# One plain pair of column blocks less in each feed-forward, and two sums moved ahead, in a two-layer hybrid decoder trunk

## The chip, the core and the metric

The kernel runs on one core of a Trainium2 chip. Its time is the device time of one execution in microseconds (us); lower is better. The five engines of the core have a queue each and run it in order: TensorE (PE) multiplies, VectorE (DVE) does elementwise work, ScalarE (ACT) activations and copies, GpSimd (POOL) some DMAs and a few splits, SyncE (SP) issues most DMAs.

## What is computed

Two layers on 512 tokens of width 1024, float32. Each layer is a feed-forward, a mixer and a feed-forward, each between two RMS norms:

```python
def swiglu(x, w_gate, w_up, w_down):
    return (jax.nn.silu(x @ w_gate) * (x @ w_up)) @ w_down
...
for layer in range(DEPTH):
    f = swiglu(rmsnorm(h, nw[0]), ffn_w_gate[layer, 0], ffn_w_up[layer, 0], ffn_w_down[layer, 0])
    h = h + FFN_RES_SCALE * rmsnorm(f, nw[1])
    u = rmsnorm(h, nw[2])
    m = even_mixer(u, ...) if layer % 2 == 0 else odd_mixer(u, ...)
    h = h + rmsnorm(m, nw[3])
    f = swiglu(rmsnorm(h, nw[4]), ffn_w_gate[layer, 1], ffn_w_up[layer, 1], ffn_w_down[layer, 1])
    h = h + FFN_RES_SCALE * rmsnorm(f, nw[5])
```

The inner width of a feed-forward is 2816, 22 column blocks of 128. The even mixer is windowed attention beside a gated delta rule, the odd one a Mamba-2 scan; the change touches neither.

## The kernel before, in words

Products are made in three passes: every operand is split into a high part (hi, made by a cast on ACT) and the rest (lo, a subtraction on DVE), and hi·hi, hi·lo and lo·hi are summed. `split` (L76 to L81) does this: the cast and the subtraction both carry lines L80 and L81. The input of a feed-forward, the normed and transposed tokens, is `uT`, a pair of tiles uhi and ulo of 128 x 4 token tiles x 8 x 128, filled by `pre` token tile by token tile as the sub-layer before ends.

`ffn` makes gate and up in three kinds of work, one behind the other:

- **Early blocks**: the first two column blocks. Each has a gate and an up product; all four run first on tokens 0 to 255, then on tokens 256 to 511 (`product`, L167 to L169, 128x256), since the last token tiles come late. `finish` (L322, L323) applies Silu and multiplies, and its result is a half of an h tile.
- **Plain blocks**: the next two column blocks, four products on all 512 tokens, 96 matmuls of 512 columns (L167 to L169).
- **Strassen units**: the rest, two column blocks at a time (gate and up of two blocks, as a 2x2 block product by seven multiplications). `block_product` (L292 to L302, matmuls at L300) is one multiplication, 24 matmuls of 256 columns, so a unit has 168. Their left operands are A11, A12, A22 (quarters of uT) and S1 to S4, sums and differences of the quarters, each with its own hi and lo. S1 to S4 are made once for each feed-forward: four sums of hi and lo (`whole`, L352), a subtraction (L362), three combinations (L363, L366, L369), four splits (s1, s2, s3, and S4, which takes the place of a quarter of uT, so its lo is called ulo). r11, r12, r21 and r22 are h tiles that aren't used yet.

A unit's weights are five loads of 512 KB: b11, t1 and t3 into the pool wq (five buffers), b21 and b22 into wraw (three). t1 and t3 are differences that an accumulating DMA of POOL (L380) makes on top of a first load by SP (L378). The block products in order: b11 with A11; b21 with A12; b11' = t1 + b22 (the `add` at L388) with S2; t1 with S1; t3 with S3; b22 with S4; b21' = b11' + b21 with A22. Each operand goes through `forms`, which splits it into whi (ACT) and wlo (DVE), four buffers of each. The q tiles hold partial results.

The order on each engine isn't written by hand: a scheduler at build time places the instructions by the order of the code and by when their inputs would be ready. On the chip each queue then runs in that order. The even mixer gives every fifth weight split to POOL, by a running count of `weights` calls (L88 to L96).

Below, the four feed-forwards are numbered first to fourth in order of time.

Of the kernel before, what the change touches and what calls it, by code (L numbers as in the profile page):

```python
# [30 lines left out]
class Trunk:  # L31
# [272 lines left out]
    def ffn(self, w_gate, w_up, w_down, post_w, next_pre, raws={}):  # L304
# [3 lines left out]
        nf = w_gate.shape[1] // 128  # L308
        tt, stt = nc.vector.tensor_tensor, nc.vector.scalar_tensor_tensor
        with ExitStack() as ctx:  # L310
            hp = ctx.enter_context(self.tc.tile_pool(name="ffn_h", bufs=1, reuse_waits="tile"))

            place = lambda dt=F32: hp.tile([128, 2, T], dt, name="h", bufs=nf // 2)
            early, plain = 2, 2
            acc, wts, hT = {}, {}, []
            with ExitStack() as ctx2:
                pool = lambda name, **kw: ctx2.enter_context(self.tc.tile_pool(name=name, reuse_waits="tile", **kw))
# [2 lines left out]
                def finish(f):  # L320
                    s = self.scratch()
                    nc.scalar.activation(s, acc[f, 0], AF.Silu)  # L322
                    tt(hT[f // 2][:, f % 2, :], acc[f, 1], s, op=OP.mult)  # L323

                r11, r12, r21, r22 = (place().rearrange("p f (k c) -> p f k c", c=128) for _ in range(4))
                for f in range(early):
                    for g, w in ((0, w_gate), (1, w_up)):
                        wts[f, g] = self.w_cols(w, f * 128, raw=raws.get((f, g)))
                        acc[f, g] = self.ps("acc" if f else "mm")
                        self.product(acc[f, g][:, :256], wts[f, g], 0, 2)  # L330
                for f in range(early):
                    for g in range(2):
                        self.product(acc[f, g][:, 256:], wts[f, g], 2, 4)
                    if f == 0:
                        hT.append(place())
                    finish(f)

                for f in range(early, early + plain):
                    if f % 2 == 0:
                        hT.append(place())  # L340
                    for g, w in ((0, w_gate), (1, w_up)):
                        acc[f, g] = self.ps("mm")
                        self.product(acc[f, g], self.w_cols(w, f * 128))
                    finish(f)


                half = lambda i, j: [u[:, 2 * i:2 * i + 2, 4 * j:4 * j + 4, :] for u in self.uT]
                A11, A12, A21, A22 = (half(i, j) for i in range(2) for j in range(2))
                flat = lambda x: x.rearrange("p t k c -> p t (k c)")

                def whole(r, x):
                    tt(flat(r), flat(x[0]).bitcast(F32), flat(x[1]).bitcast(F32), op=OP.add)  # L352

                def parts(r, x):
                    self.split(flat(r), *(flat(y) for y in x))
                    return x

                new = lambda n: [sp.tile([128, 2, KD // 2, 128], F32R, name=n + x) for x in ("hi", "lo")]
                whole(r11, A11)
                whole(r21, A21)  # L360
                whole(r22, A22)
                tt(flat(r21), flat(r22), flat(r21), op=OP.subtract)  # L362
                stt(flat(r11), flat(r21), -1.0, flat(r11), op0=OP.mult, op1=OP.subtract)  # L363
                S2 = parts(r11, new("s2"))
                S1n = parts(r21, new("s1"))
                stt(flat(r22), flat(r11), -1.0, flat(r22), op0=OP.mult, op1=OP.subtract)  # L366
                S3 = parts(r22, new("s3"))
                whole(r12, A12)
                stt(flat(r12), flat(r11), -1.0, flat(r12), op0=OP.mult, op1=OP.subtract)  # L369
                S4 = parts(r12, A21)  # L370

                def unit(f, pool, name, *parts):

                    raw = pool.tile([128, KD // 2, 256], F32, name=name)
                    for i, (w, k) in enumerate(parts):
                        src = w[k * 128:(k + KD // 2) * 128, f * 128:(f + 2) * 128].rearrange("(k p) c -> p k c", p=128)
                        if i == 0:
                            nc.sync.dma_start(raw, src)  # L378
                        else:
                            nc.gpsimd.dma_start(raw, src, accum_op=OP.add)  # L380
                    return raw

                def forms(raw):
                    hi, lo = (self.wsplit.tile([128, KD // 2, 256], F32R, name=x) for x in ("whi", "wlo"))
                    self.split(raw, hi, lo)
                    return hi, lo
# [2 lines left out]
                q = lambda n: qp.tile([128, 512], F32, name=n)  # L389

                two = lambda x: x.rearrange("p (f t) -> p f t", f=2)
                for f in range(early + plain, nf, 2):
                    b11, b21 = unit(f, wq, "wq", (w_gate, 0)), unit(f, self.wraw, "wraw", (w_gate, 4))
                    t1 = unit(f, wq, "wq", (w_gate, 0), (w_up, 0))
                    b22 = unit(f, self.wraw, "wraw", (w_up, 4))
                    t3 = unit(f, wq, "wq", (w_up, 4), (w_up, 0))
                    a = self.ps("mm")
                    self.block_product(a, forms(b11), A11, True)
                    q1 = q("q1")
                    nc.scalar.copy(q1, a)  # L400
                    c = self.ps("acc")
                    self.block_product(c, forms(b21), A12, True)
                    add(q1, c, q1)
                    nc.scalar.activation(q1, q1, AF.Silu)
                    add(b11, t1, b22)
                    self.block_product(a, forms(b11), S2, False)
                    q2 = q("q2")
                    nc.scalar.copy(q2, a)
                    d = self.ps("acc")
                    self.block_product(d, forms(t1), S1n, True)  # L410
                    q3 = q("q3")
                    nc.scalar.copy(q3, d)
                    self.block_product(a, forms(t3), S3, False)
                    add(q3, a, q3)
                    self.block_product(d, forms(b22), S4, False)
                    add(q2, d, q2)
                    hT.append(place())
                    stt(hT[-1][:, :, :256], two(q2), -1.0, two(q1), op0=OP.mult, op1=OP.mult)
                    add(b21, b11, b21)
                    self.block_product(a, forms(b21), A22, False)  # L420
                    s = self.scratch()
                    nc.scalar.activation(s, a, AF.Silu)
                    stt(hT[-1][:, :, 256:], two(q3), -1.0, two(s), op0=OP.mult, op1=OP.mult)
# [778 lines left out]
```

## Time and profile before

| | |
|---|---|
| median of 3 runs | 2156.76 us (2154.38 to 2159.07) |
| the profiled execution | 2155.31 us |
| its span, first to last instruction | 2153.5 us |
| mean granted clock of TensorE | 0.996 |
| PE busy | 2112.7 us (98%) |
| DVE busy | 1479.1 us (69%) |
| ACT busy | 1026.2 us (48%) |
| POOL busy | 149.5 us (7%) |
| DMA | 277.06 MB, mean 129 GB/s |

Times inside an execution are counted from the start of the span. A row of the timeline gives start, length, engine, line, operation, and what it writes and reads; in brackets stands how long the engine was idle before it and what ended that. Operations of one engine overlap a little, so the distance of two starts is what one costs in a chain. A matmul's length holds its way through the array; the distance of starts counts there too.

### The profile page before, as it was taken

Reading aid. Unit: us, or ns where it says so; the run is one execution under the profiler, and the core shown is the slowest. Engines: PE = TensorE matmul, PEld = TensorE weight load, DVE = VectorE, ACT = ScalarE, POOL = GpSimd, SP = SyncE. Lnnn points to the kernel's source line nnn. Section 1 sums busy time; section 2 is a strip of 40 time slices with the busy share of each in tenths; the row PEclk is TensorE's granted clock in tenths of the full one; section 3 lists DMA queues with packets and bytes.
Section 4 is the critical chain, followed back from the end, with each engine's and each line's share of the span. In section 5 each row is a group of like instructions: output and inputs, shape, how many; then the busy total and the mean of one; then the engine's idle time right before and its main releaser. Section 6 shows DMA issues by size and latency. Waiting matters only on the chain.

```text
span 2153.5 us, 33163 instructions
## 1 busy us (share of the span) xinstructions
PE 2112.7 (98%) x13311; PEld 1871.1 (87%) x13311; DVE 1479.1 (69%) x2329; ACT 1026.2 (48%) x1577; POOL 149.5 (7%) x142
## 2 busy tenths in 40 slices
PE   8999999999999999999999999999999999999998
PEld 7999988887788999988899998877778788999986
DVE  5866656869667767656686765668888846867653
ACT  4544543455563454534344455347565423544541
POOL 0011000111200011000001100000000000011000
PEclk9999999999999999999999999999999999999999
DMA  8687334342323687533658642324334236586321
GB/s 235 148 195 167 118 100 135 101 126 66 88 70 117 158 205 176 127 118 98 157 138 196 157 132 94 101 74 118 98 90 126 69 118 157 142 196 157 122 89 68
DMA packets 284037, 277.06 MB, mean 129 GB/s; under 512 B 18576, under 2 KB 244552, under 8 KB 283884
## 3 DMA queue, kind: packets, MB, share of 16 engines
q1 hardware_dynamic: 243308, 228.81, 35.0%
q0 software_dynamic: 40576, 46.14, 13.0%
q8 instruction: 104, 1.70, 0.3%
q14 instruction: 49, 0.40, 0.1%
HBM read 265.93 MB, written 4.79 MB: 126 GB/s over the span
## 4 chain that ended last, share of the span: by engine, by line
PE 84%; DVE 7%; DMA 4%; ACT 3%; issue 1%; SPq 0%; POOL 0%; DVEq 0%; ACTq 0%; POOLq 0%
PE mm L300 18%; PE acc L300 13%; PE acc L235 9%; PE acc L237 9%; PE acc L236 9%; PE mm L169 4%; PE mm L168 4%; PE mm L167 4%; DMA wraw<-in_ffn_w_up_dram 2%; DMA M<-rows_o 1%; PE acc L649 1%; DVE wlo L81 1%; PE tr L154 1%; PE acc L169 1%; PE acc L167 1%
## 5 line engine op out<-in xcount | busy, mean ns | idle before, releaser
L80 ACT CAST whi<-wraw 128x1024 fp32r<-128x1024 f32 x296 | 310.0, 1049 | 400.0 <-PE acc L237 107.4
L81 DVE TENSOR_TENSOR wlo<-wraw,whi 128x1024 fp32r<-128x1024 f32 x292 | 356.5, 1223 | 143.4 <-ACT whi L80 141.6
L167 PE MATMUL mm<-uhi,whi 128*128 128x512 f32 (+1 forms) x736 | 274.1, 373 | 1.6 <-DVE feat L476 1.3
L168 PE MATMUL mm<-ulo,whi 128*128 128x512 f32 (+1 forms) x736 | 272.9, 371 | 0.2 <-DVE ulo L81 0.2
L169 PE MATMUL mm<-uhi,wlo 128*128 128x512 f32 (+1 forms) x736 | 271.5, 369 | 0.0
L80 ACT CAST whi<-wq 128x1024 fp32r<-128x1024 f32 x144 | 150.8, 1049 | 241.4 <-issue 77.4
L81 DVE TENSOR_TENSOR wlo<-wq,whi 128x1024 fp32r<-128x1024 f32 x144 | 175.4, 1222 | 96.7 <-ACT whi L80 96.6
L235 PE MATMUL acc<-whi,hs 128*128 128x512 f32 x576 | 227.3, 395 | 0.0
L236 PE MATMUL acc<-wlo,hs 128*128 128x512 f32 x576 | 227.2, 394 | 0.0
L380 POOL DMA_DIRECT2D wq<-in_ffn_w_up_dram x72 | 92.7, 1290 | 1074.3 <-DMA wq<-in_ffn_w_gate_dram 404.0
L300 PE MATMUL mm<-uhi,whi 128*128 128x256 f32 x576 | 163.8, 284 | 3.2 <-DVE q L388 3.1
L300 PE MATMUL mm<-uhi,wlo 128*128 128x256 f32 x576 | 163.0, 283 | 0.0
L300 PE MATMUL mm<-ulo,whi 128*128 128x256 f32 x576 | 163.0, 283 | 0.0
L300 PE MATMUL acc<-uhi,whi 128*128 128x256 f32 x576 | 162.8, 283 | 0.0
L300 PE MATMUL acc<-uhi,wlo 128*128 128x256 f32 x576 | 162.8, 283 | 0.0
L300 PE MATMUL acc<-ulo,whi 128*128 128x256 f32 x576 | 162.8, 283 | 0.0
L167 PEld LDWEIGHTS mm<-uhi,whi 128*128 128x128 f32 x736 | 139.1, 189 | 26.3 <-issue 2.9
L168 PEld LDWEIGHTS mm<-ulo,whi 128*128 128x128 f32 x736 | 139.4, 189 | 25.2 <-issue 5.0
L169 PEld LDWEIGHTS mm<-uhi,wlo 128*128 128x128 f32 x736 | 139.4, 189 | 23.8 <-issue 3.6
L237 PE MATMUL acc<-whi,hs 128*128 128x512 f32 x384 | 151.5, 395 | 0.0
L236 PEld LDWEIGHTS acc<-wlo,hs 128*128 128x128 f32 x576 | 108.5, 188 | 25.3
L235 PEld LDWEIGHTS acc<-whi,hs 128*128 128x128 f32 x576 | 108.5, 188 | 25.0
(393 smaller groups left out, 5240.1 us busy)
## 6 DMA issues: line engine op xcount, KB each, us to landing
wraw<-in_ffn_w_down_dram SPq DMA_DIRECT2D x88, 512.0 KB, 3.5
wq<-in_ffn_w_gate_dram SPq DMA_DIRECT2D x72, 512.0 KB, 5.4
wq<-in_ffn_w_up_dram POOLq DMA_DIRECT2D x72, 512.0 KB, 7.6
wraw<-in_ffn_w_gate_dram SPq DMA_DIRECT2D x52, 512.0 KB, 5.4
wraw<-in_ffn_w_up_dram SPq DMA_DIRECT2D x52, 512.0 KB, 6.4
wraw<-in_odd_w_in_dram SPq DMA_DIRECT2D x40, 512.0 KB, 3.9
wq<-in_ffn_w_up_dram SPq DMA_DIRECT2D x36, 512.0 KB, 3.8
wraw<-in_even_w_in_dram SPq DMA_DIRECT2D x28, 512.0 KB, 4.3
```

The source lines that it names most:

```text
L80: nc.scalar.copy(hi, src)
L81: (nc.gpsimd if on_pool else nc.vector).tensor_tensor(lo, src, hi.bitcast(F32), op=OP.subtract)
L154: nc.tensor.transpose(p[:, j * 128:(j + 1) * 128], u[:, k * 128:(k + 1) * 128], self.ident)
L167: nc.tensor.matmul(p, whi[:, k, :], hi, start=k == 0, stop=False)
L168: nc.tensor.matmul(p, whi[:, k, :], lo, start=False, stop=False)
L169: nc.tensor.matmul(p, wlo[:, k, :], hi, start=False, stop=k == KD - 1)
L235: nc.tensor.matmul(p, ahi, hi, start=k == 0, stop=False)
L236: nc.tensor.matmul(p, ahi, lo, start=False, stop=False)
L237: nc.tensor.matmul(p, alo, hi, start=False, stop=k == nk - 1)
L300: self.nc.tensor.matmul(p[:, f * 256:(f + 1) * 256].rearrange("p (t c) -> p t c", c=128), l, r, start=new and f == k == i == 0, stop=f == ...
L380: nc.gpsimd.dma_start(raw, src, accum_op=OP.add)
L649: nc.tensor.matmul(p[:, c, :], lhs[:, c, :], rhs[:, c, :], start=True, stop=True)
```

## The change

The plain pair goes; its two column blocks become a tenth Strassen unit. `whole` and the quarters of uT are defined earlier, and the sums r11 and r12 (of the quarters of token tiles 0 and 1) are written between the two halves of the early products. r21 and r22 (token tiles 2 and 3) and all that follows stay behind them. Lines behind the plain loop get smaller numbers: the sums are L337, the subtraction L355, the combinations L356, L359 and L361, SP's loads L370, POOL's L372, the adds L380.

```diff
@@ -311,7 +311,7 @@
-            early, plain = 2, 2
+            early = 2
@@ -328,6 +328,16 @@
                         self.product(acc[f, g][:, :256], wts[f, g], 0, 2)
+
+                half = lambda i, j: [u[:, 2 * i:2 * i + 2, 4 * j:4 * j + 4, :] for u in self.uT]
+                A11, A12, A21, A22 = (half(i, j) for i in range(2) for j in range(2))
+                flat = lambda x: x.rearrange("p t k c -> p t (k c)")
+
+                def whole(r, x):
+                    tt(flat(r), flat(x[0]).bitcast(F32), flat(x[1]).bitcast(F32), op=OP.add)
+
+                whole(r11, A11)
+                whole(r12, A12)
                 for f in range(early):
                     for g in range(2):
                         self.product(acc[f, g][:, 256:], wts[f, g], 2, 4)
@@ -335,28 +345,11 @@
                     finish(f)
 
-                for f in range(early, early + plain):
-                    if f % 2 == 0:
-                        hT.append(place())
-                    for g, w in ((0, w_gate), (1, w_up)):
-                        acc[f, g] = self.ps("mm")
-                        self.product(acc[f, g], self.w_cols(w, f * 128))
-                    finish(f)
...
-                whole(r11, A11)
                 whole(r21, A21)
                 whole(r22, A22)
...
-                whole(r12, A12)
                 stt(flat(r12), flat(r11), -1.0, flat(r12), op0=OP.mult, op1=OP.subtract)
...
-                for f in range(early + plain, nf, 2):
+                for f in range(early, nf, 2):
```

What it does to the queues is shown at three places. First, DVE in the second feed-forward, before: the four sums, the S parts and the lo split of b11' (wlo_7424) behind the first plain block's L323.

```order
L323 TENSOR_TENSOR h_7195<-mm_7227,scr_7258 128x512
L352 TENSOR_TENSOR h_6964<-uhi_112,ulo_113 128x1024
L352 TENSOR_TENSOR h_6966<-uhi_112,ulo_113 128x1024
...
L362 TENSOR_TENSOR h_6966<-h_6967,h_6966 128x1024
L81 TENSOR_TENSOR wlo_7393<-wraw_7350,whi_7392 128x1024
L363 SCALAR_TENSOR_TENSOR h_6964<-h_6966,h_6964 128x1024
L81 TENSOR_TENSOR s1lo_7336<-h_6966,s1hi_7335 128x1024
...
L81 TENSOR_TENSOR s3lo_7341<-h_6967,s3hi_7340 128x1024
L369 SCALAR_TENSOR_TENSOR h_6965<-h_6964,h_6965 128x1024
L81 TENSOR_TENSOR wlo_7424<-wq_7348,whi_7423 128x1024
```

The same place in the change; wq_7314 is b11 (and then b11'), wq_7318 is t1, acc_7164 the last early product.

```order
L323 TENSOR_TENSOR h_7239<-acc_7164,scr_7291 128x512
L355 TENSOR_TENSOR h_7063<-h_7064,h_7063 128x1024
L380 TENSOR_TENSOR wq_7314<-wq_7318,wraw_7321 128x1024
L356 SCALAR_TENSOR_TENSOR h_7061<-h_7063,h_7061 128x1024
L81 TENSOR_TENSOR s1lo_7303<-h_7063,s1hi_7302 128x1024
L359 SCALAR_TENSOR_TENSOR h_7064<-h_7061,h_7064 128x1024
L81 TENSOR_TENSOR s2lo_7299<-h_7061,s2hi_7298 128x1024
L361 SCALAR_TENSOR_TENSOR h_7062<-h_7061,h_7062 128x1024
L81 TENSOR_TENSOR s3lo_7308<-h_7064,s3hi_7307 128x1024
L380 TENSOR_TENSOR q1_7355<-acc_7357,q1_7355 128x512
L81 TENSOR_TENSOR ulo_113<-h_7062,uhi_112 128x2x512
L81 TENSOR_TENSOR wlo_7390<-wq_7314,whi_7389 128x1024
```

All sums stand ahead of this piece now; the rest stands behind the last early block's L323, no longer behind the first plain block's, and the split of b11' behind all S parts.

Second, PE in the second feed-forward of the change, at the end of the second block product (acc_7357, b21 with A12); mm_7326 is the third (b11' with S2), acc_7419 the fourth (t1 with S1).

```order
L300 MATMUL acc_7357<-ulo_113,whi_7358 128x256
L300 MATMUL acc_7357<-uhi_112,wlo_7359 128x256
L300 MATMUL mm_7326<-s2hi_7298,whi_7389 128x256
L300 MATMUL acc_7419<-s1hi_7302,whi_7420 128x256
L300 MATMUL acc_7419<-s1lo_7303,whi_7420 128x256
L300 MATMUL mm_7326<-s2lo_7299,whi_7389 128x256
L300 MATMUL mm_7326<-s2hi_7298,wlo_7390 128x256
L300 MATMUL mm_7326<-s2hi_7298,whi_7389 128x256
```

Before, the third block product ran without matmuls of the fourth between; now four matmuls stand ahead of the first that reads the lo split of b11' (wlo_7390).

Third, DVE in the third feed-forward of the change, in the norm of the last token tile (ss_sum, rs_x, rs_y and rs_t are its 128x1 steps).

```order
L246 TENSOR_TENSOR scr_10519<-acc_10031,post_w_9603 128x512
L248 TENSOR_TENSOR ss_sum_10522<-ss_post_9611 128x1
L337 TENSOR_TENSOR h_10583<-uhi_112,ulo_113 128x1024
L106 TENSOR_SCALAR rs_x_10524<-ss_sum_10522 128x1
L337 TENSOR_TENSOR h_10584<-uhi_112,ulo_113 128x1024
L108 TENSOR_SCALAR rs_y_10526<-rs_x_10524 128x1
L113 SCALAR_TENSOR_TENSOR rs_t_10528<-rs_y_10526,rs_x_10524 128x1
```

Before, L248, L106, L108 and L113 follow each other there with nothing between; now the two sums stand among them.

## Rows read from the trace of the kernel before

**Rows 1.** The page: busy times with their shares, and the chain by engine.

```profile
PE 2112.7 (98%) x13311; PEld 1871.1 (87%) x13311; DVE 1479.1 (69%) x2329; ACT 1026.2 (48%) x1577; POOL 149.5 (7%) x142
...
PE 84%; DVE 7%; DMA 4%; ACT 3%; issue 1%; SPq 0%; POOL 0%; DVEq 0%; ACTq 0%; POOLq 0%
```

**Rows 2.** The chain that ended last, second feed-forward: start, length, engine, tile, line, count.

```profile
712.64 0.23 PE mm L167
...
734.43 2.87 PE mm L300 x24
737.30 2.88 PE acc L300 x24
740.18 2.85 PE mm L300 x24
...
751.60 5.76 PE mm L300 x48
```

**Rows 3.** Windows: length; PE, PEld, DVE, ACT, POOL busy (count); PEclk; DMA share; GB/s.

```profile
712.60:734.40 21.80, 21.80 (x99) 18.04 (x98) 15.11 (x14) 7.29 (x9) 1.28 (x1) 1.00 0.59 142
...
1086.60:1107.10 20.50, 20.50 (x174) 20.50 (x173) 19.00 (x20) 11.59 (x14) 1.28 (x1) 1.00 0.57 141
```

**Rows 4.** Timeline of DVE, first feed-forward, the sums and what follows.

```profile
53.34 4.62 DVE L352 TENSOR_TENSOR h<-uhi,ulo 128x1024 f32<-128x1024 f32 x4
57.88 1.22 DVE L362 TENSOR_TENSOR h<-h 128x1024 f32<-128x1024 f32 x1
...
63.56 0.68 DVE L323 TENSOR_TENSOR h<-mm,scr 128x512 f32<-128x512 f32 x1
64.16 1.22 DVE L81 TENSOR_TENSOR s2lo<-h,s2hi 128x1024 fp32r<-128x1024 f32 x1
```

**Rows 5.** Timeline of DVE, second feed-forward, during the early blocks.

```profile
700.60 1.42 DVE L81 TENSOR_TENSOR ulo<-tr,uhi 128x512 fp32r<-128x512 f32 x2 [1.46 <-ACT uhi L80]
705.40 1.23 DVE L81 TENSOR_TENSOR wlo<-wraw,whi 128x1024 fp32r<-128x1024 f32 x1 [3.39 <-ACT whi L80]
...
712.75 0.69 DVE L323 TENSOR_TENSOR h<-acc,scr 128x512 f32<-128x512 f32 x1 [0.60 <-PE acc L169]
```

**Rows 6.** Timelines of DVE and PE, third feed-forward, last token tile and early blocks.

```profile
1049.32 1.41 DVE L146 SCALAR_TENSOR_TENSOR u<-h,rs_y,pre_w 128x512 f32<-128x512 f32 x2
...
1051.11 0.27 PE L154 MATMUL tr<-ident,u 128*128 128x128 f32 x1
...
1057.59 1.22 DVE L81 TENSOR_TENSOR wlo<-wraw,whi 128x1024 fp32r<-128x1024 f32 x1 [3.50 <-ACT whi L80]
...
1064.94 0.69 DVE L323 TENSOR_TENSOR h<-acc,scr 128x512 f32<-128x512 f32 x1 [0.60 <-PE acc L169]
```

**Rows 7.** Timeline of DVE and the chain, first feed-forward.

```profile
34.12 1.23 DVE L81 TENSOR_TENSOR wlo<-wraw,whi 128x1024 fp32r<-128x1024 f32 x1 [5.64 <-ACT whi L80]
...
41.72 0.23 PE mm L167
```

**Rows 8.** Timeline of PE behind three waits, and the windows after them.

```profile
420.66 0.39 PE L198 MATMUL mm<-whi,uhi 128*128 128x256 f32 x1 [2.38 <-DVE k L81]
...
503.85 0.33 PE L847 MATMUL tr<-ident,P 128*128 128x128 f32 x1 [1.94 <-DVE h L858]
...
1451.39 0.43 PE L1072 MATMUL acc<-M,x 128*64 128x128 f32 x2 [3.35 <-DVE M L1067]
...
421.30:424.50 3.20, 3.20 (x17) 3.20 (x17) 3.00 (x16) 0.00 (x0) 0.00 (x0) 0.50 1.00 272
503.80:506.00 2.20, 2.15 (x8) 1.41 (x9) 2.18 (x10) 1.38 (x4) 0.00 (x0) 1.00 0.76 219
1452.00:1455.20 3.20, 3.20 (x8) 2.03 (x7) 0.69 (x1) 3.15 (x9) 0.00 (x0) 0.51 0.03 8
```

**Rows 9.** Timeline of POOL, second feed-forward, and the landing of its accumulating loads.

```profile
704.95 2.62 POOL L380 DMA_DIRECT2D wq<-in_ffn_w_up_dram  x2 [103.03 <-DMA wq<-in_ffn_w_gate_dram]
...
DMA to landing us min/median/max: 6.0/7.9/11.8
```

More of the change, by code (lines that the diff above doesn't have):

```diff
@@ L336, in ffn @@
                     finish(f)
-                for f in range(early, early + plain):
-                    if f % 2 == 0:
-                        hT.append(place())
-                    for g, w in ((0, w_gate), (1, w_up)):
-                        acc[f, g] = self.ps("mm")
-                        self.product(acc[f, g], self.w_cols(w, f * 128))
-                    finish(f)
[L347 to L352, printed above, removed]
                 def parts(r, x):
```

## The prediction

> **What bounds the kernel now.** I read the busy shares first: TensorE (PE) is busy 98% of the span, VectorE (DVE) 69%, and 84% of the chain that ended last is PE work, 7% DVE, 4% DMA [rows 1]. So time is saved only by fewer PE columns, and any new wait of PE adds its whole length. Then I read the stretch that the change edits. In the second feed-forward the plain pair runs from 712.64 to 734.43, 21.79 us, and the first Strassen unit follows at once [rows 2]. A unit is seven block products of 24 matmuls, of about 2.87 us each: six of them from 734.43 to 751.60, 17.17 us, and the seventh is half of the 5.76 there, together 20.05 us [rows 2]. In the pair's window DVE works 15.11 of 21.80 us on only 14 instructions, and ACT 7.29 [rows 3]. That window is where DVE makes the sums and the S parts that the first unit needs. The same instructions, hence the same two sums, stand in all four feed-forwards.
>
> **What it saves.** Each feed-forward trades a pair of 21.79 us for a unit of 20.05, so 1.74 us of PE time; four times that is 7.0 us. This is all the gain there can be.
>
> **What it takes away.** The pair was also the cover for DVE: four sums, a subtraction, three combinations and four lo splits. The diff moves two of the four sums ahead; the rest now stands directly in front of the unit that wants it. The order on DVE in the second feed-forward shows it: behind the second early block's product with its Silu (L323, which waits for the last early matmul) stand L355, the add for b11' (L380), L356, s1lo, L359, s2lo, L361, s3lo, one q add, the lo split of S4 (ulo) and only then the lo split of b11'. PE wants that split (wlo_7390) as the fifth matmul of its third block product. DVE runs its queue in order, so nothing lets that split pass.
>
> Prices: four chained 128x1024 sums take 4.62 us, and the next operation begins 4.54 us after the first, so one is 1.14 us; chained to another operation a 128x512 one is 0.60 us (63.56 to 64.16) [rows 4].
>
> *Second feed-forward.* Call the end of the early products T0; L323 starts 0.1 us after it (712.75 against 712.64) [rows 2, 5]. From T0 DVE has 0.1 + 0.60 (L323) + 8 x 1.14 (L355 to s3lo) + 0.60 (q) + 2 x 1.14 (ulo, wlo) + 0.1 to release PE = 12.8 us. PE has work that doesn't depend on it for two block products and four matmuls of 0.12 us: 5.75 + 0.48 = 6.2 us. PE idles 6.6 us. ACT stays beside it: each hi split takes about as long as its lo, and its s3hi and S4 hi stand close ahead of their lo parts, so it can add some tenths, which I leave out. Lower bound: were L323 not to hold DVE, it would run 14 operations of 1.14 and three of 0.60 from 705.40 on [rows 5], to 723.2 against 718.9, a stall of 4.3 us. I take 6.6, because L323 cannot start before T0. The two moved sums stand between the two ulo splits of the last token tile (700.60 [rows 5]), 2.3 us ahead of the second; PE's order has some 25 matmuls of 0.12 us, 3.0 us, of other products there, so I cost that at nothing; without that cover it would be up to 2.3 us.
>
> *Fourth feed-forward.* Its order on DVE is the same, so 6.6 us again.
>
> *Third feed-forward.* Here the add for b11' stands ahead, right behind the first lo split, and DVE is the limit from there: from 1057.59 [rows 6] 14 x 1.14 + 3 x 0.60 + 0.1 = 17.9, to 1075.5. T0 is 0.1 before L323's 1064.94, PE wants the split 6.2 us later, at 1071.1: 4.4 us. Besides, the two moved sums stand inside the chain of small operations that gives the last token tile's norm. They delay it by 2.28 us; its first half of u would be ready near 1050.0 (1049.32 and half of 1.41) and PE takes it up at 1051.11 [rows 6], so 1.1 us are slack and 1.2 are lost. Bounds: 0 and 2.28.
>
> *First feed-forward.* All of tile 3's splits are done early, so DVE begins with wlo at 34.12 [rows 7]: until the split of t1, which PE wants 28 matmuls into the third block, stand 15 x 1.14 + 3 x 0.60 + 0.1 = 19.0, to 53.1. PE wants it at 41.72 [rows 7] + 5.75 + 28 x 0.12 = 50.8. Stall 2.3 us.
>
> Together 6.6 + 6.6 + 5.6 + 2.3 = 21.1 us of new idle time of PE.
>
> **The clock.** PE's granted clock falls to half after some of its waits: after 2.38 us idle before 420.66 it is 0.50 from 421.3 to 424.5, and after 3.35 us before 1451.39 it is 0.51 for 3.2 us; after 1.94 us before 503.85 it stays at 1.00 [rows 8]. At 0.50, which is 1.2 of 2.4 GHz, 3.2 us of work are worth 1.6 at the full clock, so such a wait costs some 1.5 us more. Three of the four new stalls are longer than those, and I charge 1.5 each; the 2.3 us of the first feed-forward stand between the two cases, so half: 5.2 us in all. Bounds: 0 and 6.
>
> The Trainium skill, "TensorE: Matmul & The Clock Gate", section "HAM oscillation — how this bites in real kernels", says the same of waits between bursts of matmuls: each makes the clock fall again and the price of coming back is paid each time; the trace agrees at 420.66 and 1451.39 and not at 503.85. It speaks against a change that gives up a pair of blocks of unbroken work; a sum by row lengths alone, without the clock, would be 5.2 us lower.
>
> **Other edits.** The order of the loads: b21 and b22 of the first unit now stand ahead of the wq loads on SP's queue, where two plain loads stood, and come earlier than needed. t1 is late at worst: POOL issued its accumulating DMA at 704.95, and these take 6.0 to 11.8 us to land [rows 9], so from 711.0 to 716.8, while DVE wants t1 at T0 + 1.8 = 714.5; by the median of 7.9 it is there. Ten units instead of nine ask for 1.5 MB more in each feed-forward. The third feed-forward's unit stretch moves 141 GB/s at a DMA share of 0.57 [rows 3], so I charge 0.4 us for its small waits on loads and nothing elsewhere. The even mixer's weight splits shift their turn on POOL (every fifth split, by a running count); as many go there as before. Not shown by any row; bounds plus and minus 3 us, taken as 0.
>
> **Sum.** -7.0 + 21.1 + 5.2 + 0.4 = +19.7 against the profiled execution's 2155.31: 2175.0. The median of the runs, 2156.76, lies 1.45 us above that execution, inside the spread of the three runs; the sum by it would be 2176.5. I take 2175.
>
> **Rivals.**
> *The clock holds.* The stalls come but the granted clock stays at 1.00, as after 503.85: 2155.3 + 14.5 = 2169.8 (2164 to 2171 with the lower bounds of the stalls).
> *The cover is enough, only the columns count.* The mechanism: DVE had 15.11 us of work in the pair's 21.80, so it was idle for about 6.7 there, and idle too between 705.40 and 712.75 [rows 3, 5]. If that slack, together with the two block products ahead, took up the 12.8 us, PE would run on and the time would be 2155.3 - 7.0 = 2148.3, faster. It decides where DVE's chain from T0 is below 6.2 us. Against it: L323 stands ahead of the chain and waits for T0, so the slack before T0 can't be used, and the split of b11' is last in the order.
> *The two cancel.* Stalls of about 1.7 us per feed-forward, as if only the split's own place were late, give 2155.3 within 0.2%. For it speaks nothing but the errors of my sum.
> *Late loads as well.* If t1 lands at the long end in the second and fourth feed-forward (2.3 us each), DVE waits with all that is behind it, and if DVE is still behind in the second unit or the third feed-forward waits for its loads, 2183 to 2192.
>
> **How the numbers follow.** The forecast (stalls and clock, 2170 to 2183) has 0.62, the held clock 0.17, late loads 0.07, cancelling 0.07, only the columns 0.07. A measurement of this kernel can tell about 0.2%, 4.3 us, from no change. Faster is then 0.07, same 0.07, slower 0.86. The range takes the forecast, the held clock and the nearer part of late loads: 2162 to 2186. It leaves out 0.14 of the sides below, and some 0.04 above.
>
> **What would show it.** In the profile after: PE rows at L300, two block products behind the last L169 of each early stage, with idle time of about 6.6, 4.4, 6.6 and 2.3 us released by DVE s2lo and wlo; the granted clock at half for some 3 us behind them; PE's busy time lower in columns but its share of the span below 98%; DVE packed without gaps from T0 for some 12 us. The pair's 96 matmuls of 512 columns gone from each stage. It would be wrong if PE's idle time before L300 stays under 2 us in each feed-forward, or if it is released by DMA.

## The result: slower by 0.8%, and the profile after

The changed kernel takes 2174.29 us (median of 4 runs, 2171.05 to 2177.56) against 2156.95 for the kernel before (4 runs); the ratio is 1.0081, 95% interval 1.0062 to 1.0100. The forecast was 2175, in a range of 2162 to 2186.

The profiled execution has a span of 2171.6 us against 2153.5, so 18.1 us more. The page, to be read beside [rows 1]:

```profile
span 2171.6 us, 33824 instructions
...
PE 2112.7 (97%) x13599; PEld 1884.0 (87%) x13599; DVE 1507.9 (69%) x2361; ACT 1044.8 (48%) x1601; POOL 159.1 (7%) x150
...
PE 81%; DVE 9%; DMA 5%; ACT 4%; issue 2%; SPq 0%; POOL 0%; DVEq 0%; ACTq 0%; POOLq 0%
```

DVE's share of the chain rises from 7% to 9%, PE's falls from 84% to 81%. That PE's busy sum stays at 2112.7 us is chance: the missing columns take from it what, in the main, matmuls at half the clock add to it.

Where the 18.1 us came from is read off one group of matmuls, the hi·hi ones of the units at L300 with A11 and A22. Each row gives count, durations in ns, and the first and last start in us. Before, for the four feed-forwards:

```profile
L300 PE MATMUL mm<-uhi,whi x144: 277/283/283, 63.3 to 243.5; 128*128 128x256 f32 x144
...
L300 PE MATMUL mm<-uhi,whi x144: 277/283/384, 734.3 to 914.6; 128*128 128x256 f32 x144
...
L300 PE MATMUL mm<-uhi,whi x144: 278/283/387, 1086.5 to 1270.5; 128*128 128x256 f32 x144
...
L300 PE MATMUL mm<-uhi,whi x144: 277/283/386, 1841.2 to 2022.3; 128*128 128x256 f32 x144
```

And after the change:

```profile
L300 PE MATMUL mm<-uhi,whi x160: 280/283/384, 41.6 to 244.8; 128*128 128x256 f32 x160
...
L300 PE MATMUL mm<-uhi,whi x160: 278/283/386, 712.2 to 923.5; 128*128 128x256 f32 x160
...
L300 PE MATMUL mm<-uhi,whi x160: 283/283/388, 1073.8 to 1282.1; 128*128 128x256 f32 x160
...
L300 PE MATMUL mm<-uhi,whi x160: 282/283/384, 1831.1 to 2040.5; 128*128 128x256 f32 x160
```

Taking the pair's 21.79 us [rows 2] off the first start of before gives the same point in both, the end of the early products. From there to the last start, the four stages, that is the four feed-forwards, took 202.0, 202.1, 205.8 and 202.9 us before, and 203.2, 211.3, 208.3 and 209.4 after: +1.2, +9.2, +2.5, +6.5, together 19.4. The remaining -1.3 lies between them, nearly all of it (-1.6) ahead of the second feed-forward, in the stretch with the even mixer.

What stands in those stages is PE waiting in the first unit. The rows with idle time in the four first units, from the timeline of PE after the change:

```profile
48.16 0.39 PE L300 MATMUL mm<-s2lo,whi 128*128 128x256 f32 x1 [0.23 <-DVE s2lo L81]
51.83 0.39 PE L300 MATMUL mm<-s3hi,whi 128*128 128x256 f32 x1 [0.68 <-ACT q L400]
53.31 0.39 PE L300 MATMUL acc<-s1hi,wlo 128*128 128x256 f32 x1 [0.97 <-DVE wlo L81]
...
718.85 0.39 PE L300 MATMUL acc<-s1hi,whi 128*128 128x256 f32 x1 [0.56 <-ACT whi L80]
720.12 0.38 PE L300 MATMUL mm<-s2lo,whi 128*128 128x256 f32 x1 [0.77 <-DVE s2lo L81]
725.26 0.58 PE L300 MATMUL mm<-s2hi,wlo 128*128 128x256 f32 x1 [4.75 <-DVE wlo L81]
...
1084.66 0.58 PE L300 MATMUL mm<-s2hi,wlo 128*128 128x256 f32 x1 [4.48 <-DVE wlo L81]
...
1844.20 0.58 PE L300 MATMUL mm<-s2hi,wlo 128*128 128x256 f32 x1 [4.75 <-DVE wlo L81]
```

The long ones are the matmul that reads the lo split of b11', as forecast. The fourth feed-forward has the two short waits of the second as well. The idle times in the brackets are 1.9, 6.1, 4.5 and 6.1 us, together 18.5. They count from the modelled end of the matmul before. The forecast was worked out from starts; by the distance of starts, less the 0.12 us of an unhindered matmul, the same waits are 2.4, 6.7, 4.6 and 6.8 us, together 20.5 (forecast 2.3, 6.6, 4.4, 6.6: 19.9).

From some point in each of the long waits on, the clock is down. The windows (length; PE, PEld, DVE, ACT and POOL busy with counts; granted clock; DMA share; GB/s) over the slow stretches:

```profile
721.70:728.50 6.80, 3.24 (x15) 3.25 (x16) 6.80 (x7) 1.51 (x2) 0.00 (x0) 0.50 0.11 21
...
1083.50:1090.30 6.80, 5.64 (x26) 5.64 (x27) 5.65 (x5) 0.54 (x2) 0.23 (x1) 0.50 0.44 137
1841.30:1848.10 6.80, 3.90 (x18) 3.90 (x19) 6.80 (x7) 0.85 (x2) 0.00 (x0) 0.50 0.22 53
```

The clock fell while PE was still idle, so only the busy part counts: 3.2, 5.6 and 3.9 us of work at half the clock. If half of that is lost, it is 6.4 us in all; by the distance of starts the slow matmuls lose 1.6, 2.6 and 1.9 us, 6.1 in all.

The distance of successive starts at L300 gives the whole account: whatever the longer ones (over 0.14 us) have beyond 0.12 us is lost time. Summed over each stage it is 2.9, 11.2, 8.2 and 9.2 us after (31.5) against 0.0, 0.2, 3.9 and 1.0 before (5.1). That is 26.4 more; less the 7.0 that the columns give, 19.4, the number above. Of the 31.5 us, 26.9 lie in the four first units: the 20.5 of the waits, the 6.1 of the slow matmuls, and 0.3 in the matmuls right behind the short waits of the first feed-forward.

Last, the chain that ended last, second feed-forward of the change (start, length, engine, tile, line, count):

```profile
706.85 1.07 ACT L322
707.93 0.61 ACT scr L322
708.60 0.57 issue
709.17 2.35 DVE h L337 x2
711.52 0.88 DVE wlo L81
712.57 0.68 DVE h L323
713.25 1.13 DVE h L355
714.39 1.14 DVE wq L380
715.52 1.13 DVE h L356
...
722.93 1.13 DVE ulo L81
724.07 1.15 DVE wlo L81
725.26 4.31 PE mm L300 x22
```

It is DVE alone from 708.6 to 725.26, practically without a gap (the 0.57 us of issue are the rest of the first L323). It begins with the Silu of the first early block, whose table load is the 1.07 us at L322, not with the end of the early products. By a small margin: the L323 that reads the last early product starts 0.4 us behind their end (712.57 against 712.2), where 0.1 was possible before [rows 2, 5].

### The profile page after: what moved, and what is told of

It is laid out like the page before. It is cut to its first block, busy times and chain, and to the rows that moved or that the text cites. A ratio compares the mean times of both kernels' runs of the same rounds, so it can differ in the third digit from the quotient of the medians.

```text
span 2171.6 us, 33824 instructions
## 1 busy us (share of the span) xinstructions
PE 2112.7 (97%) x13599; PEld 1884.0 (87%) x13599; DVE 1507.9 (69%) x2361; ACT 1044.8 (48%) x1601; POOL 159.1 (7%) x150
## 4 chain that ended last, share of the span: by engine, by line
PE 81%; DVE 9%; DMA 5%; ACT 4%; issue 2%; SPq 0%; POOL 0%; DVEq 0%; ACTq 0%; POOLq 0%
PE mm L300 19%; PE acc L300 14%; PE acc L236 9%; PE acc L237 9%; PE acc L235 9%; PE mm L168 3%; PE mm L167 3%; PE mm L169 3%; DMA wraw<-in_ffn_w_up_dram 3%; DVE wlo L81 1%; DMA M<-rows_o 1%; PE acc L641 1%; ACT whi L80 1%; PE tr L154 1%; PE acc L1064 1%
## 5 line engine op out<-in xcount | busy, mean ns | idle before, releaser
L81 DVE TENSOR_TENSOR wlo<-wq,whi 128x1024 fp32r<-128x1024 f32 x160 | 194.8, 1221 | 110.2 <-ACT whi L80 109.8
L167 PE MATMUL mm<-uhi,whi 128*128 128x512 f32 (+1 forms) x608 | 224.0, 369 | 2.1 <-DVE feat L468 1.4
L168 PE MATMUL mm<-ulo,whi 128*128 128x512 f32 (+1 forms) x608 | 224.3, 369 | 0.2 <-DVE ulo L81 0.2
L169 PE MATMUL mm<-uhi,wlo 128*128 128x512 f32 (+1 forms) x608 | 221.2, 364 | 0.0
L300 PE MATMUL mm<-uhi,whi 128*128 128x256 f32 x640 | 182.1, 285 | 2.5 <-DVE q L380 2.5
L372 POOL DMA_DIRECT2D wq<-in_ffn_w_up_dram x80 | 102.9, 1286 | 1087.4 <-DMA wq<-in_ffn_w_gate_dram 426.6
L300 PE MATMUL mm<-uhi,wlo 128*128 128x256 f32 x640 | 181.1, 283 | 0.0
L300 PE MATMUL mm<-ulo,whi 128*128 128x256 f32 x640 | 181.1, 283 | 0.0
L300 PE MATMUL acc<-uhi,whi 128*128 128x256 f32 x640 | 181.0, 283 | 0.0
L300 PE MATMUL acc<-uhi,wlo 128*128 128x256 f32 x640 | 180.9, 283 | 0.0
L300 PE MATMUL acc<-ulo,whi 128*128 128x256 f32 x640 | 180.9, 283 | 0.0
L168 PEld LDWEIGHTS mm<-ulo,whi 128*128 128x128 f32 x608 | 115.3, 190 | 21.4 <-issue 5.7
L167 PEld LDWEIGHTS mm<-uhi,whi 128*128 128x128 f32 x608 | 114.9, 189 | 21.7 <-issue 3.3
L169 PEld LDWEIGHTS mm<-uhi,wlo 128*128 128x128 f32 x608 | 115.4, 190 | 18.2 <-issue 3.4
```

The costliest lines, as they stand in the source:

```text
L81: (nc.gpsimd if on_pool else nc.vector).tensor_tensor(lo, src, hi.bitcast(F32), op=OP.subtract)
L167: nc.tensor.matmul(p, whi[:, k, :], hi, start=k == 0, stop=False)
L168: nc.tensor.matmul(p, whi[:, k, :], lo, start=False, stop=False)
L169: nc.tensor.matmul(p, wlo[:, k, :], hi, start=False, stop=k == KD - 1)
L300: self.nc.tensor.matmul(p[:, f * 256:(f + 1) * 256].rearrange("p (t c) -> p t c", c=128), l, r, start=new and f == k == i == 0, stop=f == ...
```

## The experiments

The theory (A): the loss is the place of a few lo splits in DVE's queue, which the pair had covered. The rivals, as what makes the loss: (B) the moved sums delay what stands behind them; (C) the tenth unit itself, with its loads, is the loss; (D) DVE lacks the time in the first unit, in whatever order; (E, once the order is mended) the loads hold the units back. All runs are compared with the kernel before on the same chip. The first four ran together.

**The sums moved, the pair kept.** The definitions move with them.

```diff
 (on the kernel before)
...
+                whole(r11, A11)
+                whole(r12, A12)
                 for f in range(early):
                     for g in range(2):
                         self.product(acc[f, g][:, 256:], wts[f, g], 2, 4)
...
-                whole(r11, A11)
...
-                whole(r12, A12)
```

> The plain pair stays, only the sums r11 and r12 are moved ahead of the second half's products. Theory A (the lost cover makes the loss): the pair's 21.8 us still cover DVE, so the time is that of the kernel before, 2154 to 2159 us, and PE has no wait of over 1 us in front of any first unit. Rival B (moving the sums is itself the loss, because they stand in front of ulo and in the norm of the last token tile): 3 to 7 us slower than before, 2160 to 2164.

Measured: 2157.65 us, kernel before 2157.65, ratio 1.0008 (0.9995 to 1.0020). Moving the sums costs nothing that can be measured (the interval ends 4 us above no change), and gives nothing while the pair is there. As the cause of the 17 us, rival B falls.

**The pair gone, all sums behind the early products.**

```diff
 (on the change)
-                whole(r11, A11)
-                whole(r12, A12)
...
+                whole(r11, A11)
                 whole(r21, A21)
                 whole(r22, A22)
...
                 S3 = parts(r22, new("s3"))
+                whole(r12, A12)
```

> The pair goes, all four sums stand behind the early products in the code, as before. Theory A: DVE's chain in front of the first unit gets longer by the two sums where it had idle time before, and the lo split of b21 falls behind the S parts; by the order on DVE the stalls are about 6.5 us in the first feed-forward (2.4 in the change), 8 in the second and fourth (6.7), 4.5 in the third: 2180 to 2186 us. Rival B (the moved sums were the loss): 2168 to 2171. Rival C (the number of units, with its loads, is the loss): 2174, as the change.

Measured: 2180.13 us, ratio 1.0110 (1.0088 to 1.0132). So the second half of the change gives back some 6 us of what the first loses (2180.1 against 2174.3). In the second feed-forward PE now waits a block earlier, for the lo split of b21 (waits of PE from 715 to 745: who waited for whom, total, times, longest):

```profile
PE acc L300 <- DVE wlo L81: 6.5, 1, 6.5
```

In three of the feed-forwards the waits were shorter than I had worked out from the order (6.5 us instead of 8 here, 6.6 in the fourth; 5.1 instead of 6.5 in the first), in the third longer (6.1 instead of 4.5). The total lies at the lower end of what was expected.

**The same operations, each S part where it is needed.** The parts become a function that the first unit calls ahead of each block product:

```diff
 (on the change)
-                S2 = parts(r11, new("s2"))
-                S1n = parts(r21, new("s1"))
...
-                S4 = parts(r12, A21)
+                def S_(n):
...
                     add(b11, t1, b22)
-                    self.block_product(a, forms(b11), S2, False)
+                    w11 = forms(b11)
+                    if f == early:
+                        S2 = S_(2)
+                    self.block_product(a, w11, S2, False)
...
+                    if f == early:
+                        S1n = S_(1)
                     self.block_product(d, forms(t1), S1n, True)
```

> The change, with the same operations, but each S part is made directly ahead of the block product that reads it, and behind the split of that product's weight: only the order on DVE and ACT is another. Theory A (it is the place of the lo split of b11' in DVE's queue): the stalls shrink to 2 us in the second and fourth feed-forward, to 0.5 in the first and third, no clock falls, and the saved columns remain: 2151 to 2156 us. Rival D (DVE lacks the time in the first unit altogether, whatever the order): 2170 to 2175. Rival C (the number of units): 2174.

Measured: 2155.94 us, ratio 0.9995 (0.9980 to 1.0010), at the upper end of what was expected. Not one operation less on any engine, and 18 us less than the change: it is the order of DVE's queue (ACT's hi casts moved along with it), not the amount of its work, nor the tenth unit. Rivals C and D fall. The waits of PE in the second feed-forward (700 to 740):

```profile
PE mm L300 <- DVE s2lo L81: 1.4, 1, 1.4
PE acc L300 <- ACT whi L80: 0.6, 1, 0.6
```

No clock falls in any feed-forward. By the distance of starts the four first units lose some 7 us, as much as the columns save; so it stands where the kernel before does.

**All parts but S4's ahead of the second half.** The sums, the combinations and the splits S1 to S3 are written where the change has its two sums.

> The change, with all four sums, the combinations and the parts S1 to S3 written ahead of the second half's products; only S4's split stays behind them. Theory A: from the end of the early products DVE has L323, S4's split, the lo split of b21, the adds for b11' and b21' and the lo split of b11' to do, 7.5 us against 6.2 us of cover: stalls of 1 to 2 us in each feed-forward, 2150 to 2156 us. Rival D: 2170 to 2175. Rival B (sums and parts in front of the last token tile's splits delay the second half): a stall of 2 us or more at L167 or L168 in the second, third and fourth feed-forward, and 2156 to 2164.

Measured: 2167.20 us, ratio 1.0044 (1.0023 to 1.0065): a miss, slower than theory A's range and rival B's, though faster than rival D's. There was no wait of 2 us at L167 or L168, which rival B asked for. All S parts were early, and the lo split of b21 had moved behind them, L323 and S4's split. In the second feed-forward DVE takes it up at 719.88, and PE waits there (all waits of the execution at that place, total, times, longest):

```profile
PE acc L300 <- DVE wlo L81: 10.3, 4, 3.8
```

I had taken DVE to be through with S3 by the end of the early products; it wasn't, since three sums stood ahead of the last token tile's second ulo. This fits the theory of the queue's order, but not my count of what fits ahead of the end of the early products.

**Everything in turn.** On the third experiment:

```diff
-                whole(r11, A11)
-                whole(r12, A12)
+                whole(r11, A11)
...
                         self.product(acc[f, g][:, 256:], wts[f, g], 2, 4)
+                        if f == g == 0:
+                            whole(r21, A21)
+                            whole(r22, A22)
+                            tt(flat(r21), flat(r22), flat(r21), op=OP.subtract)
...
+                    whole(r12, A12)
                     stt(flat(r12), flat(r11), -1.0, flat(r12), op0=OP.mult, op1=OP.subtract)
                     return parts(r12, A21)
```

> As the run with the parts made in turn, and besides: r21, r22 and their difference are summed right behind the first of the second-half products, where DVE idled 2.8 us, and r12 only where S4 is made. By the order on DVE the lo splits of b21 and b11' and s2lo all end before PE wants them. Theory A: no wait of over 0.5 us in any first unit, so only the saved columns are left: about 7 us less than the kernel before of the same chip, 2148 to 2153 us if that one is near 2157. Rival E (the tenth unit's loads hold the other units back, and take what the columns give): waits for q sums behind DMA grow in the later units, 2154 to 2158.

Measured: 2153.66 us against 2157.74, ratio 0.9988 (0.9971 to 1.0005): 4 us less by the medians, but not clear of no change, and at the edge between theory A's range and rival E's. What is left of PE's waits in the second feed-forward (timelines of PE and DVE):

```profile
728.08 0.39 PE L300 MATMUL acc<-ulo,whi 128*128 128x256 f32 x1 [1.42 <-DVE ulo L81]
...
752.79 0.39 PE L300 MATMUL mm<-uhi,whi 128*128 128x256 f32 x1 [1.65 <-DVE q L385]
...
750.91 1.22 DVE L385 TENSOR_TENSOR wq<-wq,wraw 128x1024 f32<-128x1024 f32 x1 [3.21 <-DMA wraw<-in_ffn_w_up_dram]
```

The first is S4's split, which I put down to r12's late sum; that no wait of over 0.5 us would be left in a first unit was wrong. The second is rival E in the second unit: DVE's add stands and waits for a load of b22, and the q sum that PE needs is queued behind it.

**Four sums early, the rest of the change as it is.**

```diff
 (on the change)
                         self.product(acc[f, g][:, 256:], wts[f, g], 2, 4)
+                        if f == g == 0:
+                            whole(r21, A21)
+                            whole(r22, A22)
...
-                whole(r21, A21)
-                whole(r22, A22)
```

> The change, with r21 and r22 summed right behind the first of the second-half products instead of behind the early blocks' L323. The question is what starts the DVE chain in the second and fourth feed-forward. If it is the end of the early products, through L323 (as I worked it out), the work that was ahead of L323 doesn't matter and the time stays at 2172 to 2177. If DVE was already late before it (in the change it ran without a gap from the lo split of b11 on), two sums less there shorten the stalls by 2 to 3 us in the second, third and fourth feed-forward, in part with a first wait at the lo split of b21: 2161 to 2168.

Measured: 2164.28 us, ratio 1.0034 (1.0017 to 1.0051), in the second case's range. PE's waits in the second feed-forward (700 to 740):

```profile
PE acc L300 <- DVE wlo L81: 2.4, 1, 2.4
PE mm L300 <- DVE wlo L81: 1.5, 1, 1.5
```

The time is what the second case forecast, but the run doesn't decide between the two starting points of DVE's chain. The scheduler rearranged more than the sums: in this trace the subtraction, two of the combinations and s1lo also stand ahead of the last early block's L323, and the lo split of b21 and another add stand behind it. So two 128x1024 operations less, 2.3 us, stand behind L323 too, and either starting point gives the shorter wait.

**PE kept busy in the wait.** 14 matmuls that read s2lo and write a bank that nobody reads, added in the last three feed-forwards:

```diff
 (on the change)
                     self.block_product(a, forms(b11), S2, False)
+                    if f == early and not raws:
+                        dummy = self.ps("tr")
+                        x = S2[1].rearrange("p t k c -> p (t k c)").bitcast(BF16)
+                        for _ in range(14):
+                            nc.tensor.matmul(dummy, self.ident.bitcast(BF16)[:, :128], x[:, :512], start=True, stop=True)
```

> The change, with 14 matmuls of 512 bf16 columns, whose result nobody reads, on PE between s2lo and the lo split of b11' in the second, third and fourth feed-forward: some 3 us of work inside a wait of 4.5 to 4.8 us. It prices the clock. If the slow matmuls behind the stalls are the clock's fall, it stays at 1.00 there, and the time falls by what they cost, 2.2 to 2.8 us in each of the three: 2165 to 2169 us. If the clock falls all the same, the added work takes 6 us at half the clock and the time rises to 2176 to 2180. If the clock cost nothing beyond the waits: 2174.

Measured: 2169.00 us, ratio 1.0053 (1.0033 to 1.0072): 5.3 us less than the change by the medians, 6.0 by the two ratios, by more work. The intervals of the two runs overlap (the change's begins at 1.0062), so by the times alone the gain is only just visible. The timeline of PE in the second feed-forward (one of the 14 has no row) and the window over it:

```profile
721.32 2.97 PE L403 MATMUL tr<-s2lo,ident 128*128 128x512 bf16 x13
726.00 0.39 PE L300 MATMUL mm<-s2hi,wlo 128*128 128x256 f32 x1 [1.72 <-DVE wlo L81]
...
715.00:740.00 25.00, 21.89 (x166) 19.57 (x167) 23.52 (x24) 13.96 (x16) 2.55 (x2) 1.00 0.58 143
```

The matmul that waits starts 13.1 us behind the end of the early products in both kernels (726.00 less 712.9 here, 725.26 less 712.2 in the change), and the clock stays at 1.00 there and in the first units of the third and fourth feed-forward. By the distance of starts, these three units lose 5.6 us less in this trace (18.67) than in the change (24.23): PE stands as long ahead of that matmul, the useless ones included, and the slow matmuls behind it are gone. The 5.6 us are therefore the clock's part, beside the 6.1 read above. In the first feed-forward, which the edit leaves alone, the clock fell in this execution (0.50 from 54 to 56 us) behind three waits of 0.2, 0.7 and 0.9 us, which left it at 1.00 in the trace of the change.

**The version that beats both.** As "everything in turn", with r12 summed next to r21 and r22:

```diff
                             tt(flat(r21), flat(r22), flat(r21), op=OP.subtract)
+                            whole(r12, A12)
...
-                    whole(r12, A12)
                     stt(flat(r12), flat(r11), -1.0, flat(r12), op0=OP.mult, op1=OP.subtract)
```

> As the run with everything in turn, but r12 is summed with r21 and r22, where DVE idled 2 us before the end of the early products in the second and fourth feed-forward, so that S4's lo split comes 1.1 us sooner. Theory A: the wait of 1.4 us at S4's lo split in the second feed-forward goes, the waits for q sums behind late b22 loads stay: 1 to 3 us less than that run, 2150 to 2154 us, clear of the kernel before. Rival E (the loads set the pace of the units now): the time stays at 2153 to 2156, with the waits moved to q sums.

Measured: 2153.82 us against 2158.08, ratio 0.9984 (0.9973 to 0.9996). It is just clear of the kernel before, by 0.16%, though no faster than the run before it; the time lies in theory A's range and in rival E's. The waits of PE in its second feed-forward (709 to 920, all units):

```profile
PE acc L300 <- DVE ulo L81: 0.9, 1, 0.9
PE mm L300 <- DVE q L385: 0.3, 1, 0.3
PE mm L300 <- DVE s2lo L81: 0.2, 1, 0.2
```

The expectation that the wait at S4's split would go held only in part (1.4 to 0.9). Of the 7.0 us of the columns, 4.3 arrive. By the distance of starts, the units behind the first lose 9.6 us in the trace of the run before, 5.7 in this one and 5.1 in the kernel before; with one execution of each, how much of the rest is rival E's stays open.

## Why the prediction was right, and where its steps were off

The mechanism was the one that was forecast, with its places. That 2175 lies 0.7 us from the median is in part luck: the sum was 19.7 us, against 18.1 between the profiled executions and 17.3 between the medians, and it was added to the profiled execution, which lay 1.6 us below the median.

- **The columns.** 7.0 us forecast. The account by the distance of starts closes with them (31.5 - 5.1 - 7.0 = 19.4), and the last version shows that part of them can be had.
- **The lost cover.** Right in kind and place: the lo split of b11' is what PE waits for, in the second feed-forward 13.1 us behind the end of the early products where 12.8 was worked out, and the third experiment takes most of the loss away by order alone (26.9 to 6.8 us in the first units). By size, 20.5 us by the distance of starts against 19.9.
- **The reason for the size in the second and fourth feed-forward** was off. I let the chain begin at the end of the early products, because L323 waits for it, and called the earlier start the lower bound of 4.3. In fact the first lo split began at 706.65 (705.40 before, [rows 5]), L323 and its table load came next, and from 708.6 DVE had no gap; the end of the early products would have let the last L323 start 0.3 us sooner. The two starting points happen to give nearly the same end (725.0 and 725.3), and the sixth experiment, meant to tell them apart, moved both.
- **The norm of the last token tile, third feed-forward.** 1.2 us forecast; the stretch from the last unit of the second feed-forward to this stage grew by 0.2 (150.1 to 150.3 us). The term falls away; which slack took the rest I didn't test.
- **The clock.** 5.2 us forecast in all; 6.1 by the slow matmuls of the change, 5.6 by the first units of the seventh experiment. Its split was off: none in the first feed-forward (0.7 charged), and 1.6, 2.6 and 1.9 in the others (1.5 each). That the first had none may be chance: in the seventh experiment's trace the clock fell there behind waits of the same length. The rival that the clock holds falls.
- **Loads.** +0.4 forecast. Waits outside the first units lost 4.6 us after and 5.1 before: 0.5 less. The third feed-forward, which had most of them before (3.9), has 0.9 there now, the second 2.9 instead of 0.2. In the kernel before and in the change these waits are for q sums that DVE makes behind late loads of b22, and they move between stages; I didn't test what moves them.
- **The even mixer.** 0 with 3 us either way; 1.6 us less. The length of that stretch, from the last matmul of the first feed-forward's units to the end of the second's early products, goes with the pair in every trace: 468.8 us in the kernel before and 469.6 in the first experiment, which keep it, 466.9 to 467.9 in the others. That would fit the shifted splits; no run tests them apart.
- The rivals in which only the columns count, in which the two cancel, and of late t1 loads fall: the first units' waits are released by DVE and ACT, none by DMA.

## What to carry to other kernels

Before work on the busiest engine is taken out, ask what it hid: here 21.8 us of plain products were the time in which VectorE prepared the next stage, and a saving of 1.7 us a stage cost 6.6 (26.4 us in four stages). Then read the order of the queue that prepares: a short operation that is wanted first (a split of 1.14 us) stood last behind ten others, and putting each operation ahead of its reader got 18 us back with no work removed. A long wait on TensorE can be paid twice, once as idle time and once by the clock behind it: 20.5 and 6.1 us here, where the 6.1 all lie behind waits of some 4.5 us and more.

## What the runs showed of the hardware that I had not expected

The granted clock fell while PE was still waiting, but not at the same point of the wait: the stretches at 0.50 begin 1.2, 3.3 and 1.9 us after PE fell idle in the second, third and fourth feed-forward. So the length of the wait didn't tell how much work ran slow: behind 4.75 us of idle time it was 3.2 us of work in the second feed-forward and 3.9 in the fourth, behind 4.48 us it was 5.6. Nor did the length of a wait tell whether the clock falls, as the first feed-forward of the seventh experiment shows. And matmuls without use, placed in a wait, made the program faster, by some 5 us.

Executions of one kernel differ by more than the three runs at the start suggest (2150.9 to 2166.2 us in 27 runs of the kernel before). The profiled execution of the third experiment had a span of 2147.8 us where the median of its runs is 2155.94, so a single profile's total can't stand for a kernel here; what it shows of a stage's waits still serves. Some of it comes from far off the change: in the odd mixer PE waits 3.35 us for M in the trace of the kernel before [rows 8] and 3.87 in that of the change, and not at all in those of the third and the seventh experiment.
